# A decode-step kernel on one core: earlier loads of the compression weights, and copies, clearing and subtractions moved from VectorE to ScalarE and GpSimd

## The chip, the cores and the metric

The kernel runs on one core of one Trainium2 chip, in one launch. The metric is the device time of that launch in microseconds. The core has TensorE (PE; its weight loads are listed apart as PEld), VectorE (DVE), ScalarE (ACT), GpSimd (POOL) and SyncE (SP, which here only issues DMAs). Each engine takes its instructions strictly in the order in which the program was emitted for it, and an instruction that waits holds up all that stand behind it on that engine.

## The reference

One step of a decoder layer (D_MODEL 1024, one layer) for two groups that share the weights: a prompt of 1024 new tokens, and 8 samples with 8 new tokens each and a cache of 4096. `h = rms_norm(x)` is projected by `w_in`; half of the heads do stick-breaking attention, the other half NSA (attention over compressed blocks, over the best 16 blocks, and over a window). What the change touches is the compression and the cached stick-breaking attention:

```python
def stick_breaking(q, q_pos, k, v, k_pos):
    z = einsum('bqhd,bkhd->bhqk', q, k) * HEAD_DIM ** -0.5
    log_beta = where(before, log_sigmoid(z), -inf);  log_keep = where(before, log_sigmoid(-z), 0)
    a = exp(log_beta + cumsum(log_keep, axis=3, reverse=True) - log_keep)
    return einsum('bhqk,bkhd->bqhd', a, v)

def compress(rows, pe, w1, w2):                  # blocks of 32 rows, 64 wide; w1 is 2048 x 256
    blocks = rows.reshape(B, L // 32, 32, G, D) + pe[:, None, :]
    flat = blocks.transpose(0, 1, 3, 2, 4).reshape(B, L // 32, G, 32 * D)
    return silu(flat @ w1) @ w2

kc = rms_norm(compress(nsa[:, :, 0], pe_k, w1_k, w2_k), kc_g)   # nsa: 4096 cached rows and the new ones
vc = compress(nsa[:, :, 1], pe_v, w1_v, w2_v)
# NSA attends over kc, vc, over the 16 blocks picked by the compressed scores, and over 512 window rows
y = x + u @ w_out;  y = y + sigmoid(y @ w_ple_gate) * (p @ w_ple)
```

## The kernel before

Matrix products that must be exact are done in three passes: an operand is split into a high part (cast to the fp32r format) and a low part (operand minus high part), and high x high, high x low and low x high are summed. Four stages follow one another.

Phase 1 (0 to about 560 us) multiplies the normed tokens by 15 column chunks of `w_in`. `wload` loads a chunk into raw tiles (`wraw`), `wsplit` (L119 to L124) makes its high part `whi` on GpSimd and its low part `wlo` on VectorE. In the gaps `beside` runs units of the prompt's stick-breaking attention (tiles z, t, aT, u: scores on PE, three ScalarE functions L1080 to L1082, a VectorE step L1084, a scan L1085, a subtraction L1086, an exponential L1087, transposes and the product). Two pools hold phase 1's weight tiles and its small tiles (`p1w`, `p1s`); memory of closed pools is given to later tiles, and a later tile waits until the earlier owner's readers and writers are done.

The compression (about 560 to 1000 us): `c_weights` loads the two 2048x256 weights `w1` in four raw tiles on SP's queue (L436), ScalarE casts each to its high part (`w1hk`, `w1hv`, L437), VectorE subtracts for the low part (L438). `phase_c` then transposes the samples' queries (L460 to L471: tile xk from the scratch `s_qb_s`, `cQT`, an expanded copy xt, `cQc`), and `prompt` compresses the prompt's own rows: 8 blocks, each a cast `XH` (L570), a low part `XL` (L571), position columns (L574) and matmuls L500 into H. The 8 samples follow as `Batch` objects; their cached rows come by indirect DMAs that GpSimd issues (L651), and an explicit plan orders them on PE, VectorE, ScalarE and GpSimd.

The cached stick-breaking steps (`phase_b`, L1307 ff.) begin while the compression's last sample is emitted: `more` advances a clock `now` and emits every cached-step item that is due. 8 samples have 4 steps each. A step loads 8 pages of 512 KB (`bkv`, L1471 on SP), transposes the keys (L1477, VectorE), and runs scores `bz`, softplus (L1389 to L1393), a scan, an exponential, transposes and the products `bo` (L1402). `stage_d` lays the prompt's NSA units (tile nat and nsh/nwh to begin with) between these steps until about 1540 us, by due times. The output products (L1617) end the kernel. Outside of the planned part, the order on an engine is the order of emission as a scheduler with modelled costs sees it, so a changed cost or engine also shuffles neighbours.

## Time and profile before

| | us |
|---|---|
| runs of the kernel before | 1818.35, 1807.37, 1812.98 |
| their median | 1812.98 |
| profiled execution, its time | 1815.48 |
| span of that execution | 1813.7 |
| mean granted TensorE clock in it, share of full speed | 0.946 |

The span is the time from the first to the last instruction that the profiler saw; the execution's own time lies 1.8 us above it. All durations below are from this one execution. In a timeline row the first number is the start in us from the span's start, the second the duration; a row with x8 at its end is eight instructions of one form that follow one another, and its duration is theirs together. The bracket gives how long the engine was idle before it and what released it. In the windows, PEclk is the granted TensorE clock as a share of full speed, and DMA the mean busy share of the core's 16 DMA engines.

### The profile page before, as it was taken

Reading aid. Unit: us, or ns where it says so; the run is one execution under the profiler, and the core shown is the slowest. Engines: PE = TensorE matmul, PEld = TensorE weight load, DVE = VectorE, ACT = ScalarE, POOL = GpSimd, SP = SyncE. Lnnn points to the kernel's source line nnn. Section 1 sums busy time; section 2 is a strip of 40 time slices with the busy share of each in tenths; the row PEclk is TensorE's granted clock in tenths of the full one; section 3 lists DMA queues with packets and bytes.
Section 4 is the critical chain, followed back from the end, with each engine's and each line's share of the span. In section 5 each row is a group of like instructions: output and inputs, shape, how many; then the busy total and the mean of one; then the engine's idle time right before and its main releaser. Section 6 shows DMA issues by size and latency. Waiting matters only on the chain.

```text
span 1813.7 us, 41664 instructions
## 1 busy us (share of the span) xinstructions
PE 1617.2 (89%) x15742; PEld 1380.4 (76%) x15742; DVE 1244.2 (69%) x2918; ACT 874.7 (48%) x2200; POOL 598.1 (33%) x1028
## 2 busy tenths in 40 slices
PE   4899999999987699999999679998889888789998
PEld 3799888988875599899988456666667666567887
DVE  5335765866876678888888888777687786764322
ACT  3212655656665434444444367777678677211111
POOL 2124002131311255555553134444345354720000
PEclk9899999999988899999999689999899899799999
DMA  7233213232116465555554997776898771841210
GB/s 254 73 93 112 77 57 106 67 107 65 54 36 127 128 224 188 193 199 188 191 194 136 352 321 251 254 262 222 282 325 281 269 263 65 257 131 58 87 50 35
DMA packets 186898, 300.79 MB, mean 166 GB/s; under 512 B 30145, under 2 KB 100610, under 8 KB 178434
## 3 DMA queue, kind: packets, MB, share of 16 engines
q1 hardware_dynamic: 144314, 206.55, 35.1%
q0 software_dynamic: 9216, 67.11, 11.1%
q10 hardware_dynamic: 33168, 24.47, 4.2%
q8 instruction: 124, 2.03, 0.5%
q14 instruction: 76, 0.62, 0.1%
HBM read 271.81 MB, written 30.48 MB: 167 GB/s over the span
## 4 chain that ended last, share of the span: by engine, by line
PE 38%; DVE 14%; DMA 11%; ACT 6%; issue 4%; POOL 3%; SPq 1%; ACTq 0%; POOLq 0%; DVEq 0%
PE acc L1617 10%; PE H L500 5%; DMA bkv<-in_cache_sb 4%; DMA raw<-in_cache_nsa,cidx 3%; PE bo L1402 2%; PE bz L1386 2%; PE pt L1270 2%; DVE bkT L1477 2%; PE pt L1247 2%; PE acc L270 2%; ACT bAT L1528 2%; PE sc L672 2%; PE cav L814 1%; PE acc L268 1%; PE z L1201 1%
## 5 line engine op out<-in xcount | busy, mean ns | idle before, releaser
L270 PE MATMUL acc<-whi,hh 128*128 128x256 f32 (+1 forms) x704 | 204.1, 291 | 5.4 <-DVE og L1735 2.8
L270 PE MATMUL acc<-wlo,hh 128*128 128x256 f32 (+1 forms) x704 | 201.3, 287 | 0.0
L270 PE MATMUL acc<-whi,hl 128*128 128x256 f32 (+1 forms) x704 | 200.2, 289 | 0.0
L1477 DVE STREAM_TRANSPOSE bkT<-bkv 128x512 f32<-128x512 f32 x256 | 170.7, 691 | 36.0 <-DMA bkv<-in_cache_sb 29.9
L270 PEld LDWEIGHTS acc<-whi,hh 128*128 128x128 f32 x704 | 135.0, 192 | 8.2 <-POOL whi L123 3.2
L481 ACT CAST XH<-xt 128x512 fp32r<-128x512 f32 x128 | 79.1, 618 | 119.7 <-PE H L500 108.9
L270 PEld LDWEIGHTS acc<-wlo,hh 128*128 128x128 f32 x704 | 135.0, 192 | 0.2 <-issue 0.2
L270 PEld LDWEIGHTS acc<-whi,hl 128*128 128x128 f32 x704 | 133.0, 191 | 0.7 <-issue 0.3
L1238 POOL TENSOR_SCALAR t<-t,nst 128x640 f32<-128x640 f32 (+7 forms) x128 | 93.1, 729 | 114.9 <-DVE nst L1229 51.3
L123 POOL TENSOR_SCALAR whi<-wraw 128x512 fp32r<-128x512 f32 (+1 forms) x60 | 53.1, 909 | 217.6 <-PE acc L245 153.4
L1247 PE MATMUL pt<-idf,t 128*128 128x128 f32 x528 | 93.1, 294 | 20.1 <-ACT aT L1733 8.7
L1402 PE MATMUL bo<-bkv,bAT 128*16 128x128 f32 x2048 | 90.6, 297 | 21.3 <-POOL bAT L1530 13.7
L651 POOL DMA_INDIRECT raw<-in_cache_nsa,cidx x64 | 66.9, 1046 | 100.7 <-DVE xt L476 49.1
L1733 ACT COPY aT<-pt 128x512 f32<-128x512 f32 (+3 forms) x167 | 76.9, 475 | 44.6 <-PE pt L1041 20.5
L1530 POOL TENSOR_SCALAR bAT<-baT 32x128 f32<-32x128 f32 x256 | 77.2, 302 | 57.8 <-DVE baT L1520 36.8
L500 PE MATMUL H<-w1hk,XH 128*128 128x256 f32 (+1 forms) x272 | 85.7, 315 | 10.9 <-ACT XH L481 9.3
L1386 PE MATMUL bz<-bkT,bQ 128*32 128x128 f32 x2048 | 90.2, 298 | 5.1 <-DVE ba L1506 3.7
L1247 PEld LDWEIGHTS pt<-idf,t 128*128 128x128 f32 x528 | 61.0, 147 | 44.3 <-issue 18.4
L1402 PEld LDWEIGHTS bo<-bkv,bAT 128*16 128x16 f32 x2048 | 62.4, 104 | 40.4 <-POOL bAT L1530 21.6
L476 DVE STREAM_TRANSPOSE xt<-raw 128x512 f32<-128x512 f32 x132 | 88.1, 680 | 2.0 <-DMA raw<-in_cache_nsa,cidx 1.5
L1085 DVE TENSOR_TENSOR_SCAN t<-ones,t 128x1024 f32<-128x1024 f32 (+7 forms) x64 | 87.0, 1360 | 0.7
L486 POOL TENSOR_TENSOR XL<-xt,XH 128x512 fp32r<-128x512 f32 x56 | 72.1, 1287 | 38.8 <-ACT XH L481 38.5
(464 smaller groups left out, 5046.4 us busy)
## 6 DMA issues: line engine op xcount, KB each, us to landing
bkv<-in_cache_sb SPq DMA_DIRECT2D x256, 512.0 KB
wraw<-in_w_in SPq DMA_DIRECT2D x28, 512.0 KB
x<-in_x_prompt SPq DMA_DIRECT2D x8, 512.0 KB
out_sb_rows_prompt<-o ACTq DMA_DIRECT2D x32, 128.0 KB
s_gT<-og ACTq DMA_DIRECT2D x16, 256.0 KB
cwin<-in_state_win SPq DMA_DIRECT2D x8, 512.0 KB
wr<-in_w_out SPq DMA_DIRECT2D x16, 256.0 KB
g<-s_gT SPq DMA_DIRECT2D x8, 512.0 KB
```

The costliest lines, as they stand in the source:

```text
L270: nc.tensor.matmul(acc[:, :w], a[:, k, t * 128:(t + 1) * 128], b[:, k, :w], start=i == 0, stop=i == 23)
L476: V.transpose(xt[:, :, e, :, b], raw[:, :, 0:256].rearrange("p l (k e c) -> p e l k c", e=2, c=32)[:, e])
L481: S_.copy(XH.rearrange("p a b -> p (a b)"), x.rearrange("p e k b s -> p (e k b s)"))
L500: nc.tensor.matmul(H[:m, kv * 256:kv * 256 + 256], x[:, c], y[:, l * 2 + e], start=start and l + kv + e + i == 0, stop=stop and l == 7 and ...
L1085: nc.vector.tensor_tensor_scan(a[:, ::-1], K.ones.to_broadcast([128, W]), a[:, ::-1], 0.0, op0=OP.mult, op1=OP.add)
L1238: nc.gpsimd.tensor_scalar(x, x, c, 1.0, op0=OP.mult, op1=OP.mult)
L1247: nc.tensor.transpose(pt[:, b * 128:(b + 1) * 128], x, K.id)
L1386: nc.tensor.matmul(z(h, g), q(j), kT(j), start=jj == 0, stop=jj == 1, skip_group_check=True, tile_position=(0, h * 32))
L1402: nc.tensor.matmul(oav[i * 32:i * 32 + 16], lhs(g, hp), v[:, i * 128:i * 128 + 128], start=first, stop=last, skip_group_check=True, tile_p ...
L1477: V.transpose(t.kT[f][:, :, i % 4], t.k[i].rearrange("p (j c) -> p j c", j=16))
L1530: G.tensor_scalar(o, i, 1.0, 0.0, op0=OP.mult, op1=OP.add)
L1617: nc.tensor.matmul(acc, a, b, start=i == 0, stop=i == len(terms) - 1)
```

## The change

It has four parts. First, phase 1's pools are cut in four and opened in another order: small tiles first, then the weight tiles of the even chunks, those of the odd chunks, and the raw tiles. By the sizes, the compression's two raw tiles then come to lie on the raw tiles and on the odd chunks' low part, whose last user is the chunk before the last. Second, clearing moves from VectorE to GpSimd: `cbias`, `cones`, `ckz` and `cVN` in the compression, `bQ`, `bul`, `bu` in the cached steps. Third, copies move from VectorE: to ScalarE `cQT`, `cQc` (two), the expansion of the queries into `bkT`, `bQc` (two) and `bATn` (four); to GpSimd the expansion xt (now in two halves), eight small copies into `bul`, and the low parts `XL` of the prompt's 8 blocks. Fourth, `more` advances its clock by 0.3 instead of 0.5 at each call, so fewer items of the cached steps are emitted among the compression's last ones.

```diff
-        wp = P("p1w", 1)
         st = P("p1s", 1)
+        wp = [P("p1w", 1), P("p1v", 1)]
+        wr = P("p1r", 1)
...
-                raw = wp.tile([128, 4, 280], F32, name="wraw", bufs=K.nwraw)
+                raw = wr.tile([128, 4, 280], F32, name="wraw", bufs=K.nwraw)
...
-            W[c] = [raws, wp.tile([128, 8, 280], F32R, name="whi", bufs=2), wp.tile([128, 8, 280], F32R, name="wlo", bufs=2), w]
+            W[c] = [raws, *(wp[c % 2].tile([128, 8, 280], F32R, name=x, bufs=1) for x in ("whi", "wlo")), w]
...
-    V.memset(C.bias.bitcast(F32), 0.0)
+    G.memset(C.bias.bitcast(F32), 0.0)
     C.ones = cw.tile([128, 128], F32R, name="cones")
-    V.memset(C.ones.bitcast(F32), 1.0)
+    G.memset(C.ones.bitcast(F32), 1.0)
...
-    V.tensor_copy(C.QT, pq[0:64].rearrange("p (h b q) -> p b h q", h=8, b=8))
+    S_.copy(C.QT, pq[0:64].rearrange("p (h b q) -> p b h q", h=8, b=8))
...
-    V.tensor_copy(qd, qn.rearrange("t (j c) -> t j c", j=16).unsqueeze(2).to_broadcast([64, 16, 4, 32]))
+    for h in range(2):
+        x = qn[:, h * 256:h * 256 + 256].rearrange("t (j c) -> t j c", j=8).unsqueeze(2).to_broadcast([64, 8, 4, 32])
+        G.tensor_scalar(qd[:, h * 8:h * 8 + 8], x, 1.0, 0.0, op0=OP.mult, op1=OP.add)
...
-        V.tensor_copy(C.Qc[:, j0:j0 + 8].rearrange("p j t -> p (j t)"), pt)
+        S_.copy(C.Qc[:, j0:j0 + 8].rearrange("p j t -> p (j t)"), pt)
...
-                V.tensor_tensor(v[1], x, v[0].bitcast(F32), op=OP.subtract)
+                G.tensor_tensor(v[1], x, v[0].bitcast(F32), op=OP.subtract)
...
     for t in kz + [VN]:
-        V.memset(t, 0.0)
+        G.memset(t, 0.0)
...
-    V.tensor_copy(qd, qn.rearrange("t (j c) -> t j c", j=16).unsqueeze(2).to_broadcast([64, 16, 4, 32]))
+    S_.copy(qd, qn.rearrange("t (j c) -> t j c", j=16).unsqueeze(2).to_broadcast([64, 16, 4, 32]))
...
-        V.tensor_copy(Qc[:, j0:j0 + 8].rearrange("p j t -> p (j t)"), pt)
+        S_.copy(Qc[:, j0:j0 + 8].rearrange("p j t -> p (j t)"), pt)
...
-        V.memset(q, 0.0)
+        G.memset(q, 0.0)
...
-        V.memset(m, 0.0)
+        G.memset(m, 0.0)
         u = wk.tile([128, 32], F32, name="bu", bufs=2)
-        V.memset(u, 0.0)
+        G.memset(u, 0.0)
...
-            V.tensor_copy(m[h * 32:h * 32 + 32, h * 32:h * 32 + 32], u[h * 32:h * 32 + 32])
+            G.tensor_scalar(m[h * 32:h * 32 + 32, h * 32:h * 32 + 32], u[h * 32:h * 32 + 32], 1.0, 0.0, op0=OP.mult, op1=OP.add)
...
-            V.tensor_copy(ATn[:, :, :, b].rearrange("k f g h q -> k (f g) h q"), p4[:, :, :, b])
+            S_.copy(ATn[:, :, :, b].rearrange("k f g h q -> k (f g) h q"), p4[:, :, :, b])
...
-BT = [float(x) for x in "-1.5,0.5".split(",")]
+BT = [float(x) for x in "-1.5,0.3".split(",")]
```

The change adds two lines above the compression and two more in it, so that L438 of before is L440 after, and L1084 is L1088.

VectorE where phase 1 ends, before (a number at the end of a name tells tiles of one name apart):

```order
656 L1085 SCALAR_TENSOR_TENSOR t1_5303<-ones_1316,t1_5303 128x768
657 L1086 TENSOR_TENSOR t1_5303<-z_5297,t1_5303 128x768
658 L466 COPY xt_6604<-xk_6592 64x2048
659 L556 TENSOR_TENSOR cpe1_6628<-cpe_6539,cpe0_6627 128x32
660 L464 COPY cQT_1149<-H_6594 64x512
661 L1084 SCALAR_TENSOR_TENSOR t1_5340<-z_5336,t1_5340 128x384
662 L1085 SCALAR_TENSOR_TENSOR t1_5340<-ones_1316,t1_5340 128x384
663 L1086 TENSOR_TENSOR t1_5340<-z_5336,t1_5340 128x384
664 L471 COPY cQc_6591<-H_6606 128x512
665 L438 TENSOR_TENSOR w1lk_6552<-wraw_6553,w1hk_6551 128x2048
666 L471 COPY cQc_6591<-H_6616 128x512
667 L1084 SCALAR_TENSOR_TENSOR t1_5388<-z_5384,t1_5388 128x384
```

The same place after the change:

```order
653 L1088 SCALAR_TENSOR_TENSOR t1_5309<-z_5303,t1_5309 128x768
654 L1089 SCALAR_TENSOR_TENSOR t1_5309<-ones_1322,t1_5309 128x768
655 L1090 TENSOR_TENSOR t1_5309<-z_5303,t1_5309 128x768
656 L440 TENSOR_TENSOR w1lk_6560<-wraw_6561,w1hk_6559 128x2048
657 L440 TENSOR_TENSOR w1lk_6560<-wraw_6568,w1hk_6559 128x2048
658 L480 STREAM_TRANSPOSE xt_6649<-raw_6640 128x4x4x32 x2
659 L560 TENSOR_TENSOR cpe1_6637<-cpe_6547,cpe0_6636 128x32
660 L1088 SCALAR_TENSOR_TENSOR t1_5346<-z_5342,t1_5346 128x384
661 L1089 SCALAR_TENSOR_TENSOR t1_5346<-ones_1322,t1_5346 128x384
662 L1090 TENSOR_TENSOR t1_5346<-z_5342,t1_5346 128x384
663 L1088 SCALAR_TENSOR_TENSOR t1_5394<-z_5390,t1_5394 128x384
```

The clearing, the copy into xt, `cQT` and `cQc` are gone from the row; both subtractions for `w1lk` and the transposes of the prompt's rows (xt from raw) now stand ahead of the attention units' L1088, where they stood behind them.

GpSimd in the same place, before (L631 prepares a sample's queries, L651 issues an indirect load of cached rows):

```order
137 L574 TENSOR_SCALAR XL_6644<-cpe1_6628 128x4
138 L631 TENSOR_SCALAR cQb0_1150<-cQc_6591 32x2x32 x8
139 L651 DMA raw_6900<-in_cache_nsa,cidx_1163 128x2048
140 L574 TENSOR_SCALAR XH_6661<-cpe0_6627 128x4
141 L574 TENSOR_SCALAR XL_6662<-cpe1_6628 128x4
142 L574 TENSOR_SCALAR XH_6679<-cpe0_6627 128x4
143 L574 TENSOR_SCALAR XL_6680<-cpe1_6628 128x4
144 L651 DMA raw_6902<-in_cache_nsa,cidx_1163 128x2048
```

And after:

```order
138 L470 TENSOR_SCALAR xt_6612<-xk_6600 64x1024 x2
139 L578 TENSOR_SCALAR XH_6652<-cpe0_6636 128x4
140 L635 TENSOR_SCALAR cQb0_1156<-cQc_6599 32x2x32
141 L578 TENSOR_SCALAR XH_6670<-cpe0_6636 128x4
142 L578 TENSOR_SCALAR XL_6653<-cpe1_6637 128x4
143 L575 TENSOR_TENSOR XL_6653<-xt_6649,XH_6652 128x4x64
144 L578 TENSOR_SCALAR XL_6671<-cpe1_6637 128x4
145 L575 TENSOR_TENSOR XL_6671<-xt_6649,XH_6670 128x4x64
146 L635 TENSOR_SCALAR cQb0_1156<-cQc_6599 32x2x32 x7
147 L655 DMA raw_6909<-in_cache_nsa,cidx_1169 128x2048
148 L655 DMA raw_6911<-in_cache_nsa,cidx_1169 128x2048
```

The expansion xt stands ahead of the queries and loads, two `XL` subtractions (L575) stand between them, and the two indirect loads follow each other; before, the second stood behind the position columns of two more blocks. Six more subtractions follow the loads.

TensorE where the cached steps open, before (sA and sB are the compression's score tiles, L1386 and L1402 the scores and products of the cached steps, L1014 transposes of nat):

```order
5845 L1014 MATMUL pt_12943<-idf_75,nat_12940 128x128 x4
5846 L1386 MATMUL bz_11927<-bkT_11914,bQc_11765 32x32 x32
5847 L1014 MATMUL pt_12953<-idf_75,nat_12950 128x128 x4
5848 L1386 MATMUL bz_12068<-bkT_12041,bQ0_11786 32x128 x16
5849 L735 MATMUL sA_11512<-idf_75,ckn_11515 64x128
5850 L735 MATMUL sA_11512<-idf_75,ckn_11516 64x128
5851 L1153 MATMUL pt_12960<-idf_75,kcn_12917 128x32
5852 L741 MATMUL sA_11512<-ckT_11901,cQT_1149 64x256
5853 L1437 MATMUL bpt_11994<-idf_75,ba_11973 32x128 x4
5854 L974 MATMUL pt_13003<-idf_75,nat_13001 128x128 x4
5855 L1386 MATMUL bz_12068<-bkT_12066,bQ0_11786 32x128 x16
5856 L1402 MATMUL bo_12287<-bvn_11841,bATn_11842 16x128 x4
```

And after:

```order
5844 L1018 MATMUL pt_12580<-idf_75,nat_12577 128x128 x4
5845 L739 MATMUL sA_11521<-idf_75,ckn_11524 64x128
5846 L739 MATMUL sA_11521<-idf_75,ckn_11525 64x128
5847 L1390 MATMUL bz_11949<-bkT_11923,bQc_11774 32x32 x25
5848 L745 MATMUL sA_11521<-ckT_11890,cQT_1155 64x256
5849 L1390 MATMUL bz_11949<-bkT_11923,bQc_11774 32x32 x7
5850 L1018 MATMUL pt_12590<-idf_75,nat_12587 128x128 x4
5851 L1390 MATMUL bz_12099<-bkT_12065,bQ0_11795 32x128 x16
5852 L765 MATMUL sA_11521<-cSc_11926,cRs_1288 16x64 x4
5853 L847 MATMUL sB_11739<-idf_75,cSg_11937 128x64 x2
5854 L1157 MATMUL pt_12597<-idf_75,kcn_12554 128x32
5855 L1441 MATMUL bpt_12016<-idf_75,ba_11995 32x128 x4
```

The compression's last transposes and scores (L739, L745, L765, L847) now stand ahead of the first step's second half of the scores, and L739 no longer stands behind the last transposes of nat.

## Rows read from the trace of the kernel before

**Rows 1.** the page, its head and part 1.

```profile
span 1813.7 us, 41664 instructions
...
PE 1617.2 (89%) x15742; PEld 1380.4 (76%) x15742; DVE 1244.2 (69%) x2918; ACT 874.7 (48%) x2200; POOL 598.1 (33%) x1028
```

**Rows 2.** windows: length, busy (xcount) of PE, PEld, DVE, ACT, POOL; PEclk, DMA, GB/s.

```profile
550.00:600.00 50.00, 35.49 (x234) 27.78 (x232) 35.68 (x45) 31.27 (x54) 9.26 (x20) 0.80 0.76 162
600.00:650.00 50.00, 36.26 (x293) 33.24 (x294) 32.66 (x63) 18.70 (x37) 17.32 (x25) 0.90 0.43 142
1000.00:1050.00 50.00, 32.61 (x552) 24.14 (x553) 43.08 (x120) 19.76 (x55) 9.57 (x27) 0.64 0.99 347
1050.00:1100.00 50.00, 38.82 (x581) 29.16 (x575) 43.53 (x108) 30.83 (x87) 19.92 (x51) 0.83 0.91 301
```

**Rows 3.** timeline of SP's DMA issues, end of phase 1: start, us, what.

```profile
563.04 4.73 SPq L436 DMA_DIRECT2D wraw<-in_cmp_w_k  x8
568.40 10.23 SPq L562 DMA_DIRECT2D raw<-out_nsa_rows_prompt  x11
```

**Rows 4.** timeline of ScalarE, same stretch; in brackets idle time before, and its releaser.

```profile
586.12 1.90 ACT L437 CAST w1hv<-wraw 128x2048 fp32r<-128x2048 f32 x1 [3.45 <-DMA wraw<-in_cmp_w_v]
...
595.69 1.90 ACT L437 CAST w1hv<-wraw 128x2048 fp32r<-128x2048 f32 x1 [3.02 <-DMA wraw<-in_cmp_w_v]
```

**Rows 5.** timeline of VectorE, same stretch.

```profile
570.13 1.22 DVE L466 COPY xt<-xk 64x2048 f32<-64x2048 f32 x1 [2.79 <-DMA xk<-s_qb_s]
...
575.63 2.28 DVE L438 TENSOR_TENSOR w1lk<-wraw,w1hk 128x2048 fp32r<-128x2048 f32 x1
...
579.46 1.30 DVE L476 STREAM_TRANSPOSE xt<-raw 128x512 f32<-128x512 f32 x2 [0.48 <-DMA raw<-out_nsa_rows_prompt]
...
583.92 0.40 DVE L571 TENSOR_TENSOR XL<-xt,XH 128x256 fp32r<-128x256 f32 x1
...
585.30 0.55 DVE L1086 TENSOR_TENSOR t<-z,t 128x384 f32<-128x384 f32 x1
...
605.52 1.21 DVE L1085 TENSOR_TENSOR_SCAN t<-ones,t 128x512 f32<-128x512 f32 x1
...
615.89 0.29 DVE L1735 COPY u<-pt 128x128 f32<-128x128 f32 x1 [1.24 <-PE pt L1097]
```

**Rows 6.** timeline of GpSimd, same stretch.

```profile
575.80 2.22 POOL L631 TENSOR_SCALAR cQb<-cQc 32x64 f32<-32x64 f32 x1 [4.00 <-DVE cQc L471]
578.60 2.04 POOL L631 TENSOR_SCALAR cQb<-cQc 32x64 f32<-32x64 f32 x7 [0.58 <-DVE cQc L471]
...
594.35 0.97 POOL L651 DMA_INDIRECT raw<-in_cache_nsa,cidx  x1 [1.69 <-PE H L500]
...
615.94 0.62 POOL L661 TENSOR_SCALAR cvs<-raw 128x512 f32<-128x512 f32 x1 [7.58 <-PE pt L1097]
...
629.00 1.27 POOL L486 TENSOR_TENSOR XL<-xt,XH 128x512 fp32r<-128x512 f32 x1 [8.68 <-ACT XH L481]
```

**Rows 7.** chain of waits, same stretch.

```profile
619.67 6.52 DMA ckz<-s_win_s
```

**Rows 8.** timeline of VectorE where the cached steps open.

```profile
991.97 1.03 DVE L1341 MEMSET bQ<- 128x512 f32 x2 [1.33 <-PE H L500]
...
995.85 1.21 DVE L1332 COPY bkT<-bs 64x2048 f32<-64x2048 f32 x1
...
998.54 0.69 DVE L1338 COPY bQc<-bpt 128x512 f32<-128x512 f32 x1
999.26 0.73 DVE L1364 COPY bul<-bu 32x32 f32<-32x32 f32 x4
...
1014.92 0.86 DVE L1441 COPY bATn<-bpt 32x128 f32<-32x128 f32 x4
```

**Rows 9.** timeline of SP, same stretch.

```profile
995.24 33.53 SPq L1471 DMA_DIRECT2D bkv<-in_cache_sb  x23
```

**Rows 10.** chain of waits, same stretch.

```profile
997.41 10.53 DMA nat<-s_win_p
```

## The prediction

> **What bounds the kernel now.** I read the page first: PE is busy 89% of the span [rows 1], so over the whole only PE's own gaps can give time. Then the windows, to find the gaps beside the change. Two stretches fall short of that 89%: 550 to 650 us, where PE works 35.49 and 36.26 of 50 us at a granted clock of 0.80 and 0.90, and 1000 to 1100 us, where it works 32.61 and 38.82 at 0.64 and 0.83 [rows 2]. Neither has another engine that is full: in the first VectorE is busy 35.68 and 32.66 of 50, so the limit there is a chain of waits, while in the second VectorE is busy 43.08 and 43.53 and the DMA engines 0.99 and 0.91 [rows 2], so two resources compete to be the limit. Last I read the timelines of these two stretches, engine by engine, and the chain of waits. The change touches nothing else: up to the end of phase 1, through the samples' compression and in the output products the instructions stand in the same order.
>
> **First stretch, what goes.** SP issues the first compression weights at 563.04 and the raw prompt rows only behind them, at 568.40 [rows 3]. The weights of the second kind come behind those again, and ScalarE sat idle 3.45 and 3.02 us for them, casting at 586.12 and 595.69 [rows 4]; no block of the prompt is complete without these casts. After the change the first weights lie in memory that is free when the chunk before the last is done, so SP gets them out during the last chunk, 4.73 us of issuing leave the place where the raw rows wait, and the rows can go at about 563 (568.40 less 4.73 is 563.7). The rows' transposes, and the loads of the second weights, which wait for the first `w1lk` subtraction, move up by about as much.
>
> VectorE loses, of the work that stands before or between the attention units: the copy xt 1.22 with an idle wait of 2.79 for xk ahead of it; three copies of 512 columns, taken at the 0.69 of the one in rows 8; eight subtractions `XL` at 0.40 [rows 5, 8]; some clearing under 1 us. That is 1.2 + 2.1 + 3.2 = 6.5 us of work. But the wait does not go with the work. The transposes of the raw rows now stand ahead of the next unit's step on VectorE, so the engine waits there for the last of eight raw loads instead. The 11 loads of rows 3 took 10.23 us to issue, 0.93 each; the eighth was out at 575.8 and the transposes began at 579.46 [rows 5], 3.6 later. Eight from 563.7 end at 571.1; with 3.6 to land and 1.30 to transpose the units go on at 576.0. The copy xt ends at 571.4 in before, so some 4 us are lost at the head. They are won back behind it: both `w1lk` subtractions (2.28 each), the transposes and the copies then no longer lie between the units. The two units that follow have six steps, four at 0.55 and two scans, which at 1.21 for 512 columns [rows 5] are 0.91 for 384: 4.0 us, so they end at 580.0, where the last of them ended at 585.30 + 0.55 = 585.9 in before [rows 5].
>
> The end of this stretch is the last unit's copy u at 615.89 [rows 5]. Bounds for what it gains: below, a loss of 4 us, if that later start is what counts and the work taken from VectorE lay beside waits; above, 12 us, the distance by which the last cast can move (from 595.69 to about 583). I take **5.5 us**, near the 5.9 of those two units, since the later ones stand in a chain with ScalarE that the change does not shorten. Behind that end the next is late at once: the chain waits 6.52 us for `ckz` [rows 7], whose clearing moves to GpSimd and may come earlier, but the gate values' loads on ScalarE's queue, which follow the units, end in the same place. I put nothing for it.
>
> **What it adds.** ScalarE gets three copies at about 0.6; it is idle for 18.7 of 50 us there [rows 2], and I put nothing. GpSimd gets two halves of xt. It has no such row; per element it took 0.62 us for 512 columns with one input [rows 6], so 1024 columns are an estimated 1.24, both 2.5, against 1.22 on VectorE: 1.3 us later for what follows (queries, then the indirect loads), in exchange for a second indirect load that no longer waits until 594.35 [rows 6]. And eight subtractions: 512 columns with two inputs took 1.27 [rows 6], so 256 are an estimated 0.64 instead of 0.40 each. From below, they cost less than nothing, since on VectorE they queued behind scans of 1.21 [rows 5]. From above, they meet those scans anyway: a GpSimd copy of 32x64 took 2.22 at 575.80, where seven of its kind took 2.04 together; it ended at 578.02, just behind the VectorE subtraction of 575.63 to 577.91 [rows 5, 6]. So GpSimd stands still while VectorE runs an instruction with two inputs in SBUF, and one subtraction may take 0.64 + 1.21 = 1.85 us.
>
> The Trainium skill (SBUF — State Buffer, "Who interferes with whom") says why: the second of VectorE's SBUF inputs comes through the read port that it shares with GpSimd, and whoever comes second is blocked for the whole instruction. The trace agrees, 0.29 to 2.22. By that rule the moved subtractions are not free of VectorE; read alone it speaks against this part of the change, since each `XL` on GpSimd can also hold up a scan. The section also says that plain fp32 copies on VectorE can take that pair, so their removal works the other way; no row here shows that separately.
>
> **Second stretch, what goes.** From VectorE: `bQ` 1.03, the expansion 1.21, `bQc` twice 0.69, the small copies twice 0.73, `bATn` 0.86 [rows 8], and the small clearing, about 0.3: 6.2 us. VectorE is busy 43 of 50 us there [rows 2], so most of this is on the path until the steps are in full swing. What it goes to is idle: ScalarE is busy 19.76 and GpSimd 9.57 of 50 [rows 2]. ScalarE's expansion is estimated at the 1.90 of the cast with as many columns [rows 4], and it stands ahead of the next loads of nat, 1.9 us later for a load that took 10.53 [rows 10].
>
> What is late next are the page loads: 23 of them took 33.53 us [rows 9], 1.46 us each, and a step needs eight, 11.7 us. Where a step waits for its pages, VectorE's relief is worth nothing.
>
> The clock of 0.3 puts the compression's last scores ahead of the first step's second half on TensorE, and its products `cav` ahead of the second step's second half. The first step's own chain comes out at about the same time, and the prompt's units, which fill TensorE's gaps between the steps, begin about two steps' products earlier. In before PE idles 17.4 and 11.2 us in these two windows, 28.6 of 100; at 89% it would idle 11. Bounds: above, 12 us, two thirds of the surplus of 17.6; below, a loss of 8, if the reshuffling costs the first steps half a step's loads and more. I take **6.5 us**, near the 6.2 that leave the busiest engine, and put the reordering at the rest, 0.3.
>
> **The sum.** 1815.48 is the time of the profiled execution. Less 5.5 and 6.5 that is 1803.5. The profiled execution lies 2.5 us above the median of 1812.98, so against the median the forecast is **1801 us**.
>
> **Rivals.** (a) No change, about 1812: the waits only change their names. In the first stretch the raw rows on VectorE stand where xk stood, in the second the page loads set the pace. For it speak the 0.99 of the DMA engines [rows 2]; against it, that PE idles 17.4 us there and VectorE hardly ever. That the weights don't load early, because another owner of their memory is late, falls under this too: then 4.7 us less in the first stretch.
>
> (b) Slower, about 1823: GpSimd becomes the bound of the prompt's blocks. xt 2.5, queries of 2.22 and 2.04, two indirect loads of 0.97 and eight subtractions at up to 1.85 make 2.5 + 4.3 + 1.9 + 14.8 = 23.5 us, in order, with position columns between them; if each of the eight comes in front of a block's matmuls late by 1.45 (1.85 less 0.40), that is 11.6 us, and the second stretch gives at most what the reshuffling takes. 1813 + 11.6 less 2 for the relief of VectorE is 1823. It decides from the point where the waiting per subtraction passes 0.7 us (5.5 us over eight). Against it: GpSimd is busy only 9.26 and 17.32 of 50 us [rows 2]. Read alone, the rule of the Trainium skill named above makes this the expected way; without it the case stands on the 2.22 us of rows 6.
>
> (c) A larger gain, about 1790: both upper bounds nearly, 11 and 12 us, the clock rising with the fuller TensorE. For it speaks the granted clock of 0.64 where PE now waits [rows 2].
>
> **How the numbers follow.** The forecast gets 0.60, with a range of its own of 1793 to 1808; (c) 0.12, (a) 0.17, (b) 0.11. A measurement of this kernel tells about 0.5%, 9 us, from no change, so faster means below 1804. Of the forecast 0.43 lies below that, 0.15 within and 0.02 above: faster 0.43 + 0.12 = 0.55, same 0.17 + 0.15 = 0.32, slower 0.11 + 0.02 = 0.13. The range of 1788 to 1815 leaves out (b), the outer part of (c), and a little of the forecast.
>
> **What would show it.** In the trace after: weights for `w1hk` issued before 558 and its casts done by 570; the casts of `w1hv` before 585; the last copy u between 606 and 614; `XL` on GpSimd at 0.6 to 1.9; the second indirect load before 590. At the opening: VectorE below 42 of 50 us, PE above 35 in the first window, nsh and nwh of the prompt's units done earlier against the first step. The forecast is wrong if the last copy u is not earlier, if the page loads still stretch over as long and PE idles as before, or if the time won is idle again further on, between 1100 and 1540.

## The result, and the profile after

The changed kernel takes 1802.87 us (median of 12 runs, 1794.72 to 1808.24) against 1815.33 us for the kernel before (12 runs beside it): a ratio of 0.9933, 95% interval 0.9916 to 0.9951. That is 12.5 us less; 1801 was forecast. The profiled execution has a span 17.3 us shorter, 4.8 more than the medians: it lies 4.7 us under the median of its kernel. One run of all that are told of here, of the kernel called e7_xl_back below, took 2994.80 us and counts in no ratio. Head and part 1 of the page after:

```profile
span 1796.4 us, 41633 instructions
...
PE 1605.1 (89%) x15742; PEld 1377.6 (77%) x15742; DVE 1229.5 (68%) x2880; ACT 879.0 (49%) x2210; POOL 608.1 (34%) x1057
```

PE is again busy 89%, with 12.1 us less busy time for the same number of matmuls [rows 1]. The windows that answer to those of before:

```profile
550.00:600.00 50.00, 39.23 (x276) 31.84 (x275) 36.80 (x40) 32.76 (x59) 20.22 (x36) 0.83 0.56 121
600.00:650.00 50.00, 37.29 (x284) 33.25 (x283) 28.17 (x53) 18.64 (x36) 19.11 (x27) 0.86 0.45 149
1000.00:1050.00 50.00, 33.35 (x560) 25.89 (x560) 44.12 (x115) 22.38 (x65) 9.79 (x27) 0.70 0.99 335
1050.00:1100.00 50.00, 41.58 (x575) 31.37 (x575) 38.48 (x119) 35.25 (x107) 24.21 (x55) 0.93 0.82 284
```

The first stretch holds more PE work; its clock is 0.83 instead of 0.80 in the first window and 0.86 instead of 0.90 in the second. At the opening PE went from 32.61 to 33.35 and from 38.82 to 41.58 [rows 2], while VectorE did not fall in the first window (44.12) and fell by 5 us in the second. The first stretch in detail, SP's issues, ScalarE and VectorE:

```profile
497.63 19.94 SPq L438 DMA_DIRECT2D wraw<-in_cmp_w_k  x8
563.05 5.10 SPq L566 DMA_DIRECT2D raw<-out_nsa_rows_prompt  x10
568.91 1.79 SPq L438 DMA_DIRECT2D wraw<-in_cmp_w_v  x4
...
573.80 5.22 SPq L566 DMA_DIRECT2D raw<-out_nsa_rows_prompt  x5
```

```profile
564.62 3.70 ACT L439 CAST w1hk<-wraw 128x2048 fp32r<-128x2048 f32 x2
...
577.23 1.90 ACT L439 CAST w1hv<-wraw 128x2048 fp32r<-128x2048 f32 x1 [2.45 <-DMA wraw<-in_cmp_w_v]
...
583.00 1.90 ACT L439 CAST w1hv<-wraw 128x2048 fp32r<-128x2048 f32 x1 [3.45 <-DMA raw<-out_nsa_rows_prompt]
...
610.47 11.63 ACTq L611 DMA_DIRECT2D cgtc<-s_br_s  x8
622.19 1.28 ACT L510 ACT_TABLE_LOAD   x1 [11.15 <-DMA cgtc<-s_br_s]
```

```profile
566.61 5.32 DVE L440 TENSOR_TENSOR w1lk<-wraw,w1hk 128x2048 fp32r<-128x2048 f32 x2
571.85 1.29 DVE L480 STREAM_TRANSPOSE xt<-raw 128x512 f32<-128x512 f32 x2
...
573.16 0.54 DVE L1088 SCALAR_TENSOR_TENSOR t<-z,t 128x384 f32<-128x384 f32 x1
...
577.28 0.56 DVE L1090 TENSOR_TENSOR t<-z,t 128x384 f32<-128x384 f32 x1
...
584.63 1.31 DVE L480 STREAM_TRANSPOSE xt<-raw 128x512 f32<-128x512 f32 x2 [3.17 <-DMA raw<-out_nsa_rows_prompt]
585.86 2.25 DVE L440 TENSOR_TENSOR w1lv<-wraw,w1hv 128x2048 fp32r<-128x2048 f32 x1
...
601.39 0.29 DVE L1739 COPY aT<-pt 128x128 f32<-128x128 f32 x1 [4.29 <-PE pt L1045]
...
613.10 0.29 DVE L1739 COPY u<-pt 128x128 f32<-128x128 f32 x1 [4.21 <-PE pt L1101]
```

The weights now go out at 497 to 518 and the raw rows at 563.05 instead of 568.40 [rows 3]; the casts `w1hv` came at 577.23 and 583.00 instead of 586.12 and 595.69 [rows 4]; the attention units went on at 573.16, and the second of them ended at 577.84 instead of 585.85 [rows 5]. But the last copy u came at 613.10, only 2.8 us earlier. The 8 us were lost again to new waits: five raw rows now stand behind the second weights (issued from 573.80), and VectorE idles 3.17 us for them. ScalarE idles 3.45 us; the bracket names the same rows, but the cast that waits reads the weights issued from 571.95. Then VectorE idles 4.29 and 4.21 us for PE. The chain of waits shows what stands between (`raw` on POOL is the second indirect load, L504 the matmuls of the prompt's blocks):

```profile
578.71 5.60 DMA raw<-out_nsa_rows_prompt
...
586.21 2.71 POOL raw L655
...
590.23 2.40 PE H L504 x10
...
593.61 5.88 PE H L504 x48
```

GpSimd:

```profile
567.97 4.86 POOL L470 TENSOR_SCALAR xt<-xk 64x1024 f32<-64x1024 f32 x2 [19.60 <-DMA xk<-s_qb_s]
...
573.66 0.73 POOL L575 TENSOR_TENSOR XL<-xt,XH 128x256 fp32r<-128x256 f32 x1
...
578.79 1.15 POOL L655 DMA_INDIRECT raw<-in_cache_nsa,cidx  x1 [0.29 <-POOL cQb L635]
586.21 2.71 POOL L655 DMA_INDIRECT raw<-in_cache_nsa,cidx  x1 [6.27 <-DVE xt L480]
```

The eight `XL` took 0.73 each or so, none was held up by a scan; two scans were held up by an `XL` instead (last section). The second indirect load went out at 586.21 instead of 594.35 [rows 6], but it took 2.71 us. Behind the last unit the chain has the same wait as in [rows 7], as forecast:

```profile
615.50 6.31 DMA ckz<-s_win_s
```

At the opening, the first cached step's softplus (L1397) in the kernel after, and the first of the prompt's 64 units to reach its reciprocal (L1232):

```profile
1017.69 0.65 DVE L1397 SCALAR_TENSOR_TENSOR bs<-bz,ba 128x512 f32<-128x512 f32 x1
...
1058.04 0.13 DVE L1232 RECIPROCAL nst<-nst 128x3 f32<-128x3 f32 x1
```

The latter in the kernel before:

```profile
1075.06 0.18 DVE L1228 RECIPROCAL nst<-nst 128x3 f32<-128x3 f32 x1
```

And SP's store of the compression's last sample, before and after:

```profile
1059.86 0.71 SPq L870 DMA_DIRECT2D s_on_s<-co  x1
```

```profile
1039.71 0.71 SPq L874 DMA_DIRECT2D s_on_s<-co  x1
```

The first step itself is 1 us earlier (1018.75 in before), the compression's end 20 us and the first unit 17 us. From the last sample's silu (992 and 988) to the last unit's reciprocal, one window each for before and after:

```profile
992.00:1544.10 552.10, 469.32 (x6754) 357.07 (x6752) 435.15 (x1218) 378.44 (x1110) 230.86 (x527) 0.91 0.77 261
```

```profile
988.00:1525.60 537.60, 454.95 (x6754) 352.56 (x6752) 427.47 (x1197) 382.19 (x1117) 232.25 (x543) 0.92 0.79 268
```

Here lies the gain: of 17.3 us in the span, 2.8 come up to the copy u, 1.2 from there to the silu, and 14.5 from this stretch of the cached steps; the output products give 1.2 back. Cut at the first unit's reciprocal, the stretch is, before and after:

```profile
992.00:1075.10 83.10, 55.74 (x849) 41.93 (x847) 73.64 (x209) 35.48 (x95) 20.10 (x64) 0.69 0.96 319
1075.10:1544.10 469.00, 413.58 (x5906) 315.14 (x5905) 361.51 (x1010) 342.95 (x1016) 210.76 (x464) 0.95 0.74 251
```

```profile
988.00:1058.00 70.00, 46.87 (x735) 35.49 (x733) 59.40 (x174) 35.13 (x93) 19.50 (x67) 0.76 0.96 316
1058.00:1525.60 467.60, 408.08 (x6019) 317.07 (x6019) 368.07 (x1024) 347.06 (x1025) 212.75 (x477) 0.94 0.76 260
```

So 13.1 of the 14.5 us lie between the last silu and the first unit, the opening, where VectorE is the busiest engine: 114 matmuls fewer stand there. The units' stretch behind it takes 113 more and is 1.4 us shorter.

Over both, PE's gaps are as long as before, 552.1 - 469.3 = 82.8 and 537.6 - 455.0 = 82.6 us. The same 6754 matmuls were busy for 14.4 us less, at a granted clock of 0.92 instead of 0.91. At two levels, 1.2 and 2.4 GHz, 0.91 means 18% of the time at the lower one, 99 us, and 0.92 16%, 86 us, each good to some 5 us, since the view gives two digits. With PE busy some 85% of that time and half as fast, 13 us less at the lower level are worth about 5.5 us, and by the play of the digits anything from 1 to 10. By tile, the busy time fell most for the units' scores z (94.83 to 89.50 us) and the steps' scores bz (91.48 to 87.51), then for cav, bo and pt by 1.5 to 1.7 each; what shortened them beyond the clock is not shown. Matmuls overlap in this count (the 2112 of bz, 0.24 us each or more, make 91.48 us), so some that merely stand closer together also make it smaller.

### The profile page after: what moved, and what is told of

It is laid out like the page before. It is cut to its first block, busy times and chain, and to the rows that moved or that the text cites. A ratio compares the mean times of both kernels' runs of the same rounds, so it can differ in the third digit from the quotient of the medians.

```text
span 1796.4 us, 41633 instructions
## 1 busy us (share of the span) xinstructions
PE 1605.1 (89%) x15742; PEld 1377.6 (77%) x15742; DVE 1229.5 (68%) x2880; ACT 879.0 (49%) x2210; POOL 608.1 (34%) x1057
## 4 chain that ended last, share of the span: by engine, by line
PE 37%; DVE 15%; DMA 13%; ACT 7%; issue 3%; POOL 3%; SPq 1%; ACTq 0%; DVEq 0%; POOLq 0%
PE acc L1621 11%; DMA bkv<-in_cache_sb 6%; PE H L504 6%; DMA raw<-in_cache_nsa,cidx 3%; PE acc L270 2%; DVE bkT L1481 2%; PE pt L1274 2%; PE bo L1406 2%; PE acc L272 2%; PE sc L676 1%; PE bz L1390 1%; PE pt L1251 1%; PE cav L818 1%; ACT bAT L1532 1%; DVE bs L1400 1%
## 5 line engine op out<-in xcount | busy, mean ns | idle before, releaser
L504 PE MATMUL H<-w1hk,XH 128*128 128x256 f32 (+1 forms) x272 | 85.9, 316 | 8.8 <-ACT XH L485 7.8
L1390 PE MATMUL bz<-bkT,bQ 128*32 128x128 f32 x2048 | 86.1, 301 | 4.2 <-DVE ba L1510 2.8
```

Source lines behind the costliest of these rows:

```text
L504: nc.tensor.matmul(H[:m, kv * 256:kv * 256 + 256], x[:, c], y[:, l * 2 + e], start=start and l + kv + e + i == 0, stop=stop and l == 7 and ...
L1390: nc.tensor.matmul(z(h, g), q(j), kT(j), start=jj == 0, stop=jj == 1, skip_group_check=True, tile_position=(0, h * 32))
```

## The experiments

Theory: the forecast's two stretches each give their part, and the reordering at the opening lets the units fill PE's gaps earlier. Rivals: one part makes the whole gain; or the order that the scheduler happens to lay in the cached stretch moves the time by itself. Ratios are against the kernel before on the same chip; the quotient of two medians can differ from them by up to 0.002. The other columns are us in the profiled execution of each: `last u`, in brackets counted from phase 1's last copy u, which starts anywhere between 559.0 and 566.5 (564.22 in before), though phase 1 is the same in all but for its pools; `store`; `opening`, from the last sample's silu to the first unit's reciprocal; `units`, from the first to the last reciprocal. Single executions of one kernel lie up to 9 us from their median, so the ratios decide and the other columns show where to look.

| kernel | ratio (95%) | last u | store | opening | units |
|---|---|---|---|---|---|
| before | 1 | 615.9 (51.7) | 1059.9 | 83.1 | 469.0 |
| all parts | 0.9933 (0.9916 to 0.9951) | 613.1 (49.0) | 1039.7 | 70.0 | 467.6 |
| e1_first | 1.0069 (1.0048 to 1.0090) | 614.7 (50.6) | 1053.4 | 80.8 | 483.2 |
| e2_open | 1.0024 (1.0003 to 1.0044) | 613.4 (52.0) | 1042.7 | 70.8 | 485.1 |
| e3_clock | 1.0005 (0.9981 to 1.0028) | 614.8 (52.2) | 1046.3 | 72.4 | 475.3 |
| e4_open_clock | 0.9974 (0.9951 to 0.9997) | 611.5 (52.5) | 1037.6 | 67.3 | 481.3 |
| e5_after_clock05 | 1.0055 (1.0035 to 1.0074) | 612.1 (48.7) | 1057.5 | 79.2 | 481.5 |
| e6_first_clock | 1.0020 (1.0001 to 1.0038) | 614.8 (49.0) | 1046.2 | 70.5 | 481.1 |
| e7_xl_back | 0.9954 (0.9935 to 0.9973) | 615.9 (51.6) | 1039.5 | 68.3 | 472.8 |
| e8_after_clock04 | 1.0029 (1.0007 to 1.0051) | 613.7 (48.8) | 1047.2 | 78.4 | 483.7 |
| e9_no_pools | 1.0064 (1.0041 to 1.0087) | 619.0 (52.4) | 1044.6 | 69.0 | 498.2 |
| e10_after_clock025 | 0.9975 (0.9956 to 0.9993) | 612.4 (50.3) | 1034.1 | 68.6 | 483.8 |
| e11_tiny_copy | 0.9972 (0.9954 to 0.9991) | 613.2 (49.1) | 1035.7 | 67.4 | 471.7 |
| b1_gates_early | 0.9886 (0.9867 to 0.9905) | 611.2 (48.3) | 1025.5 | 62.0 | 481.0 |

**The parts alone and in pairs.** e1_first is the kernel before with the change's part up to `ckz`, e2_open with its part in `phase_b`, e3_clock with the last line only, e4_open_clock with the last two. e5_after_clock05 and e6_first_clock are the remaining pairs:

```diff
 # e1_first: all up to G.memset(t, 0.0) for ckz, cVN     # e2_open: from S_.copy(qd, ...) to ATn
 # e3_clock:
-BT = [float(x) for x in "-1.5,0.5".split(",")]
+BT = [float(x) for x in "-1.5,0.3".split(",")]
 # e4_open_clock: e2_open and e3_clock.  e5_after_clock05: e1_first and e2_open.  e6_first_clock: e1_first and e3_clock.
```

> Only the first stretch is changed: the pools in the new order, and the compression's clearing, copies and low parts XL moved; the cached steps and the clock of 0.5 stay. Theory: the last unit's copy u comes at about 613 instead of 615.89, the time won is 3 us and is kept to the end, a ratio of 0.998 (0.996 to 1.000). Rival, that the whole gain of 12 us comes from here and only shows later: ratio 0.993.

> Only the cached steps' own clearing and copies are moved off VectorE (bQ, bul, bu, the expansion, bQc, bATn); pools, compression and the clock of 0.5 stay. Theory: VectorE is the busiest engine at the opening and its 6.2 us are worth about 4 us: ratio 0.998 (0.995 to 1.000), the last sample's store s_on_s some 4 us earlier than 1060. Rival, that only the order of items counts: ratio 1.000, the store within 2 us of 1060.

> Only the clock of the emission is changed from 0.5 to 0.3; nothing is moved between engines. Theory: the compression's tail goes ahead of the first steps, the store s_on_s comes 10 us earlier or more, and the whole gains about 5 us: ratio 0.997 (0.994 to 1.000). Rival 1, that only VectorE's relief counts: ratio 1.000. Rival 2, that the order alone makes the whole of the second stretch's gain: ratio 0.995 and no more from the moves beside it.

> The cached steps' moves and the clock of 0.3 together, the first stretch as before. Theory: about 9 us, ratio 0.995 (0.993 to 0.997), the sum of the two alone; the store s_on_s near 1043. Rival, that the two cover the same wait: no better than the better one alone. Rival, that without the first stretch nothing is won: 1.000.

> The changed kernel, but with the emission clock of 0.5 as before: all moves, no reordering by the clock. Theory (order decides): with 0.5 the moves were slower in both halves, 1.0069 and 1.0024, so together about 1.009 (1.004 to 1.012), and the lost time lies between the first cached step and the 17th, which take over 260 us. Rival (the moves work once they are complete): about 0.995, the clock adding only the 0.0005 less that it showed alone.

> The first stretch's part (pools, compression's moves) with the clock of 0.3; the cached steps' own clearing and copies stay on VectorE. Theory (the order that 0.3 gives lets the first stretch's 3 to 4 us through): 0.997 (0.995 to 0.999). Rival (parts add up): 1.0069 and 1.0005 make 1.007.

My theory failed for each part alone, for e6, and narrowly for e4 (0.9974 against 0.993 to 0.997); e5 came as expected. The first stretch's part was to gain 3 us and made the kernel slower by 0.7%, 10 us by the medians; the opening's moves were to gain 4 us and lost a little, though the store came 17 us earlier; the clock alone changed nothing, though the store came 13.5 us earlier. Only opening and clock together gain alone, 0.26%. No part makes the gain, and the parts don't add up: the three alone multiply to 1.0098, together they are 0.9933. What the clock of 0.3 is worth depends on what is moved with it: nothing without moves, 0.005 with either half (1.0024 to 0.9974, 1.0069 to 1.0020), 0.012 with both (1.0055 to 0.9933). The loss of e1_first lies in the cached stretch; its window, as above:

```profile
988.30:1552.30 564.00, 476.06 (x6754) 361.50 (x6752) 437.29 (x1219) 382.06 (x1111) 231.59 (x528) 0.90 0.75 257
```

564.0 us, 11.9 longer than before; 6.7 of it in PE's busy time for the same matmuls, 5.2 in gaps, at a clock of 0.90; all of it lies behind the first unit. In this window nothing was moved to another engine in e1_first; only the order in which the scheduler laid steps and units can have changed, the time at which the stretch began, and, since the pools are others, where later tiles lie in memory. In e2_open the opening is 12.3 us shorter and the units' stretch 16.1 longer:

```profile
989.00:1059.80 70.80, 46.81 (x799) 36.49 (x799) 61.44 (x176) 36.59 (x97) 20.93 (x71) 0.78 0.95 321
1059.80:1544.90 485.10, 414.98 (x5957) 318.24 (x5955) 374.01 (x1021) 347.21 (x1021) 214.08 (x471) 0.95 0.74 251
```

The clock of the emission alone (e3_clock) shortens the opening by 10.7 us, and all nine kernels with 0.3 or 0.25 have one of 62.0 to 72.4; with 0.5 or 0.4 only e2_open has. That part of the gain comes back from kernel to kernel. The units' stretch, 467.6 to 498.2, then keeps it or takes it away.

**XL back, and a clock between.**

```diff
 # e7_xl_back, against the changed kernel
-                G.tensor_tensor(v[1], x, v[0].bitcast(F32), op=OP.subtract)
+                V.tensor_tensor(v[1], x, v[0].bitcast(F32), op=OP.subtract)
 # e8_after_clock04, against the changed kernel
-BT = [float(x) for x in "-1.5,0.3".split(",")]
+BT = [float(x) for x in "-1.5,0.4".split(",")]
```

> The changed kernel with the prompt blocks' low parts XL back on VectorE; nothing else. Theory: GpSimd's eight subtractions of 0.7 us cost nothing and gain 1 us at most, so 0.994 against the kernel before (0.992 to 0.996), last copy u within 2 us of 613.1. Rival (VectorE held the prompt's blocks up): last u 2 to 4 us later, ratio 0.996. Rival (any edit shuffles the order of the cached steps): the first stretch the same, but the whole off by 5 us or more in either direction.

> The changed kernel with a clock of 0.4 in place of 0.3. Theory (an order that lets the compression's tail go first is what counts): still about 0.994 if the store s_on_s stays before 1045, else between 0.994 and 1.009. Rival (the gain at 0.3 is one lucky order): anything between 0.993 and 1.009 with the store as early as at 0.3, the steps 1 to 17 taking 255 us or more.

With `XL` on VectorE the last u came 2.8 us later (2.6 from phase 1's last copy), as the rival had it (VectorE held the blocks up):

```profile
615.90 0.29 DVE L1739 COPY u<-pt 128x128 f32<-128x128 f32 x1 [4.83 <-PE pt L1101]
```

The ratios' intervals of e7 and of the changed kernel overlap, so `XL`'s 3 us are seen in the trace of the stretch and not proven at the end. A clock of 0.4 lost the whole gain and 0.3% more. Its store was 56.5 us behind the silu and its first unit 78.4, against 51.7 and 70.0 at 0.3, so neither side was clean: the order was a different one, and slower.

**The pools, and the clock once more.** e9_no_pools is the changed kernel with phase 1's four pool lines as before. e10_after_clock025 has "-1.5,0.25".

> The changed kernel with phase 1's pools as before: the raw compression weights load late again, all other moves and the clock of 0.3 stay. Counted in the order on TensorE, the compression's last product cav stands behind 0.31 of a cached step's products, as in the three kernels that were faster than before so far (all parts 0.9933, XL back 0.9954, moves at the opening with clock 0.3 0.9974); where it stands behind 0.56 or more the moved kernels took 1.000 to 1.007. Theory (this place decides, and the early weights are worth 3 us on top): 0.995 (0.993 to 0.997), the last copy u about 3 us later than the 613.1 of the changed kernel. Rival (orders are luck): anything from 0.993 to 1.007.

> The changed kernel with a clock of 0.25 in place of 0.3: on TensorE the compression's last product cav stands behind 0.08 of a cached step's products instead of 0.31, the first unit of the prompt behind 0.6 as at 0.3. Theory (the earlier the compression's tail is through, the earlier the units fill the gaps): 0.993 or a little less (0.989 to 0.995). Rival (0.3 is one lucky order among many): 0.996 to 1.003, though the store s_on_s is as early as at 0.3 or earlier.

Without the pools, SP's issues of the first weights and the last u:

```profile
565.45 4.49 SPq L436 DMA_DIRECT2D wraw<-in_cmp_w_k  x8
```

```profile
618.97 0.29 DVE L1737 COPY u<-pt 128x128 f32<-128x128 f32 x1 [1.07 <-PE pt L1099]
```

The weights load late as in before, and the last u is 5.9 us later than with the pools; phase 1's last copy was 2.5 us later already, so 3.4 us are the pools'. With the pools or with `XL` undone the last u is back at the 51.6 to 52.5 us of the kernels that lack the whole part: the gain up to there needs both. But the kernel takes 1.3% longer, 22 us, and the theory that the place of the last `cav` decides is dead: it is the same as in the changed kernel. An early place goes with the gain all the same: of the seven kernels that have the last `cav` there or earlier (all parts, e4, e7, e9, e10, e11, b1) six are faster than before, and of the six other changed ones none is. The cached stretch took 567.2 us:

```profile
994.10:1561.30 567.20, 478.50 (x6754) 361.46 (x6752) 432.25 (x1198) 384.62 (x1118) 232.54 (x542) 0.90 0.75 255
```

With the same moves and the same clock as the changed kernel it is 29.6 us longer, 23.5 of that in busy time and 6.1 in gaps. At 0.90, 20% of 567 us lie at the lower level, 113 against 86, each good to some 5 us. The whole of the 29.6 us lies behind the first unit. The pools' memory is long given back by then; whether it is the order or the other places of later tiles that costs this, no run separates. e10 has the earliest store of all but the last kernel and still gives only 0.25%, as its rival had it: earlier is not always better.

**A neutral edit.**

```diff
     C.Qc = cw.tile([128, 16, 64], F32, name="cQc")
+    S_.copy(cw.tile([128, 1], F32, name="cnop"), K.id[:, 0:1])
```

> The changed kernel with one more instruction: a ScalarE copy of one column (128x1) that nothing reads, put where the compression opens. It costs about 0.2 us of an engine that is idle there, and no data, load or engine of any other instruction changes; but the scheduler, whose modelled times it shifts, lays the cached steps and the prompt's units in another order from there on (of ScalarE's rows between the first and the last difference about half stand elsewhere, as many as against the kernel before). Theory (the order of the cached stretch by itself moves the time by as much as the change does): a ratio to before off from the changed kernel's 0.9933 by 0.003 or more in either direction, 0.996 to 1.004 the likeliest, with the time up to 990 us unchanged and the difference between 990 and 1540. Rival (the moves and the clock are worth what they showed): 0.993 (0.991 to 0.995).

The ratio is 0.9972, 0.4% off the changed kernel's, with intervals that don't meet. But the medians (1804.12 and 1802.87) differ by 0.07% only, the kernel before being faster beside it (1809.26), and the profiled execution, the fastest of twelve and 9 us under their median, shows the cached stretch as short as the changed kernel's:

```profile
986.90:1526.00 539.10, 457.05 (x6754) 350.78 (x6752) 429.65 (x1199) 382.09 (x1118) 232.53 (x542) 0.92 0.80 268
```

So it stays open whether that order costs anything; the changed kernel was not run beside it. Half of ScalarE's rows in this stretch stand elsewhere, and the stretch need not be longer: not every new order is a bad one. The twelve executions of this one program also show the clock at work without any change of order: 1794.8 and 1797.5 us at a mean granted clock of 0.953, 1805.9 and 1806.8 at 0.944.

**A version that beats both.** ScalarE issues the eight gate loads for 11.63 us, and its table load waits 11.15 for them; the prompt's silu and what follows it in the compression stand behind both. They need nothing of that stretch:

```diff
+    C.gtc = cw.tile([64, 8, 3], F32, name="cgtc")
+    for h in range(8):
+        nc.sync.dma_start(C.gtc[h * 8:h * 8 + 8], hbm(T["br_s"], h * 3, [[24, 8], [192, 8], [1, 3]]))
...
-    gtc = wk.tile([64, 8, 3], F32, name="cgtc")
-    for h in range(8):
-        nc.scalar.dma_start(gtc[h * 8:h * 8 + 8], hbm(T["br_s"], h * 3, [[24, 8], [192, 8], [1, 3]]))
+    gtc = C.gtc
```

> The changed kernel with the eight small loads of the gate values (cgtc) issued on SP's queue where the compression opens, instead of on ScalarE's behind the last attention unit, where ScalarE issues them for 11.6 us and its table load waits 11.2. Theory: the prompt's silu comes 3 to 8 us earlier than 623.5 and the kernel takes 0.990 of before (0.986 to 0.994), unless the load of ckz, 6.3 us in the chain, ends at the same time as before; then 0.993. Its order puts the last cav behind 0.06 of a step, so if early tails help it gains there too; if orders are luck, it may lose what it gains here (up to 1.000).

SP issues them in 5.35 us, in a gap of its own, and ScalarE's silu starts at 612.12 instead of 623.49, more than the 3 to 8 us expected (1.2 us of it phase 1 had ahead):

```profile
558.66 5.35 SPq L461 DMA_DIRECT2D cgtc<-s_br_s  x8
```

```profile
610.82 1.28 ACT L513 ACT_TABLE_LOAD   x1 [1.69 <-PE pt L1102]
612.12 0.59 ACT L513 ACTIVATE chs<-H 64x512 f32<-64x512 f32 x1
```

0.9886 against before, 21 us. Of the 11 us won here 7.4 are left at the last sample's silu (980.6) and 2 at the last unit: the cached stretch gave 5.5 back. These two executions lie 2.9 us above and 4.7 us under their medians, which differ by 12 us, on two chips. A new order came with this edit too, so the 11 us at the prompt's silu are shown as the loads', and what became of them behind it is not.

## Why the prediction was right, and where it was not

The total was right: 1801 forecast, 1802.87 measured, faster as the likeliest case. Its two terms, 5.5 and 6.5, were not.

*The first stretch*, 5.5 forecast, 2.8 in the trace, 2.6 from phase 1's last copy. Right: early weights, raw rows at 563 (563.7 forecast), casts before 570 and 585, `XL` between 0.6 and 1.9, second indirect load before 590, last u between 606 and 614. The units even went on 3 us before the forecast 576.0. The step that failed is the one that let the two units' gain (5.9 forecast, 8.0 measured) stand to the end: the second half of the raw rows, GpSimd's indirect load and PE's blocks became the next waits. The rival without the pools (e9) shows that the early weights are worth about 3.4 us up to the last u.

*The opening*, 6.5 forecast as the work that leaves VectorE. The sign set for it failed: VectorE was busy 44.12, not below 42, in the first window, PE 33.35, not above 35. Yet the opening became 13.1 us shorter. The moves alone do 12.3 of that (e2_open), the clock of the emission alone 10.7 (e3_clock): they cover the same wait, and the reordering, which I had put at 0.3 us, was mis-sized. The step that failed is again the one to the end. The sum has no term for the units' stretch behind the opening, and there e2_open lost 16.1 us (ratio 1.0024) and e3_clock 6.3 (1.0005); the two together without the first stretch kept 0.26%, all parts 0.67%. Nor did PE's gaps fill, as I had thought: they stayed at 83 us.

*The rivals.* (a) fell for the whole. (b), GpSimd as the bound, fell by the 0.73 us of `XL` and the u at 613.1, though GpSimd's indirect load and `XL` do stand in the chain from 586.21 to 590.23; slower by 10 us did come true, in e1_first, but in the cached stretch and not at the place I priced. (c) fell.

What is shown: with the reordering the opening takes 62.0 to 72.4 us instead of 83.1, in nine kernels. From the last silu to the last unit, opening included, the kernels take between 537 and 567 us with almost the same matmuls (6748 to 6754 records), and edits far ahead of it move it by more than they move their own stretch; these are single executions, but the ratios by and large follow them. Its length goes with PE's busy time, less with its gaps (73.8 us in e7_xl_back, 94.1 in e2_open) and loosely with the granted clock (551.6 us at 0.93 in e6_first_clock, 537.6 at 0.92 after the change). What stays open: which property of an order makes the units' stretch short. The first unit's start does not suffice (e9 and the changed kernel start units 69 and 70 us behind the silu, and take 498 and 468 from the first to the last), nor does the place of the last `cav`. That the agreement of the total with the forecast owes something to chance follows from this: the first term came to half and the second to twice its size, in executions whose spans differ by more than the medians, and the same two terms would have forecast e5 and e9 as faster.

## What to carry to other kernels

Where a scheduler lays the order, a small edit buys its own stretch and a new order of all that follows; time the parts together and apart before crediting one of them, and expect a loss or gain of up to a per cent that no term of the edit names. A term that is read from a stretch should be carried on to the next wait that ends in it, which here halved it. Small loads that an engine issues itself cost that engine time: move them to a queue that is idle, ahead of where they are needed.

## What the hardware showed beyond that

GpSimd and VectorE took turns where the VectorE instruction has two inputs in SBUF and GpSimd reads there too. The second `w1lk` subtraction and the second half of xt in the kernel after, and the two halves in e9_no_pools, where VectorE ran no such instruction beside them:

```profile
568.80 3.12 DVE L440 TENSOR_TENSOR w1lk<-wraw,w1hk 128x2048 fp32r<-128x2048 f32 x1
569.76 3.07 POOL L470 TENSOR_SCALAR xt<-xk 64x1024 f32<-64x1024 f32 x1
```

```profile
572.25 2.05 POOL L468 TENSOR_SCALAR xt<-xk 64x1024 f32<-64x1024 f32 x2 [21.39 <-DMA xk<-s_qb_s]
```

By itself a half of xt took 1.04 us (2.5 for both was the estimate, 2.05 is what they take) and a `w1lk` subtraction 2.28 [rows 5]. Beside each other the first half ended at 569.78 (1.81 us from 567.97), 0.9 behind the first subtraction, the second subtraction at 571.92, 2.1 behind that half, and the second half at 572.83, 0.9 behind that subtraction: 6.22 us from 566.61 on, against 6.61 for the four one after the other. The Trainium skill (SBUF — State Buffer, "Who interferes with whom") lets the second of two such instructions wait for the whole of the first; the trace agrees, each waited for the one before it, and running side by side gained next to nothing.

The moved subtractions held up scans in the same way:

```profile
573.74 1.46 DVE L1089 TENSOR_TENSOR_SCAN t<-ones,t 128x384 f32<-128x384 f32 x1
```

Beside the `XL` of 573.66 this scan took 1.46 us, against 0.96 for the next of its size at 576.29, and the one of 640 columns at 590.57, beside another `XL`, 1.81 against 1.48 in before.

The indirect load at 586.21 took 2.71 us of GpSimd; it ran beside the `w1lv` subtraction of 585.86 to 588.11 and ended 0.8 us behind it. Of the other 63 half took 0.99 or less, and the six that took 1.28 to 1.46 each began while VectorE ran an `XL` subtraction of 0.67 to 0.69 us.

ScalarE took 1.45 us to issue each gate load (11.63 for eight), SP 0.67 (5.35 for eight) for the same transfers at another time.
